# Two first loads placed ahead of their engines' register set-up, in a convolution with a residual add

## The chip, the cores and the metric

The kernel runs on one core of one Trainium2 chip. The metric is the device time of one execution in microseconds (us), lower is better. A run counts as slow here when its time is more than 1.5% above the fastest of the same kernel.

## The reference

A 3x3 convolution with padding 1, 16 images of 64 channels and 64x64 points to 64 channels, and then a residual added:

```python
"x": np.random.randn(16, 64, 64, 64).astype(np.float32),
"weight": np.random.randn(64, 64, 3, 3).astype(np.float32) * 0.1,
"residual": np.random.randn(16, 64, 64, 64).astype(np.float32),
...
output[b, co] += weight[co, ci, kh, kw] * x_pad[b, ci, kh:kh+h, kw:kw+w]
...
return (output + residual).astype(np.float32)
```

## The kernel before

SyncE issues the image loads, the weights, the residual loads and the stores; ScalarE issues the first residual load, and packs images as bf16; TensorE multiplies; VectorE adds the residual in place. The part that matters here is how two loads are issued. Each is issued as any other, then a helper takes it out of its place and inserts it into the first block of the program, ahead of the barrier with which all engines begin:

```python
def to_the_front(dma):
    ...
    front = nc.main_func.blocks[0].instructions
    here = nc.cur_bb.bb.instructions
    ins = here.pop()
    assert ins.name == dma.ins.name
    at = next(
        i for i, e in enumerate(front) if e.engine == ins.engine and isinstance(e, mybir.InstDrain)
    )
    front.insert(at, copy.replace(ins, ins=[fixed(a) for a in ins.ins], outs=[fixed(a) for a in ins.outs]))
...
# on SyncE
to_the_front(load_x(p))                       # the first image load, p == 0: 128 partitions x 16 KB
nc.sync.dma_start(out=wraw[:, :], in_=w_rows[:, :]).then_inc(s_w, 16)
...
# on ScalarE
to_the_front(load_ro(0, nc.scalar))           # the first residual load: 128 partitions x 16 KB
```

The first block, as printed while the kernel was traced, has for SyncE and ScalarE five register moves and a load of a base register each, then the barrier (a drain, a semaphore wait and a branch, of which the trace has records on all five engines). The drain is what the helper looks for.

## Time and profile before

| what | before |
|---|---|
| time, median (range) of 3 runs | 122.44 us (122.42 to 122.47) |
| span of the profiled run | 120.5 us |
| bytes moved, rate from 3.5 to 117 us | 50.48 MB, 431 GB/s |
| busiest compute engine | TensorE, 72% of the span |
| first image load, first residual load issued | 0.00 us, 0.12 us |
| first bytes | after 1.0 us |

The span counts from the first record, so a load at 0.00 us is itself that first record. Engine names with a q (SPq, ACTq) are the engines' sequencers, which issue transfers and run register, semaphore and branch instructions. In the lines of the profile PE is TensorE, DVE VectorE, ACT ScalarE, POOL GpSimd and SP SyncE; DMA stands for the 16 engines that carry the transfers; xr is the buffer of the images, ro that of the residual and the output, wraw that of the weights. The lines themselves stand in the prediction below.

### The profile page before, as it was taken

To read this page: it belongs to the slowest core of one execution; us is meant where nothing else is said; L and a number is where in the kernel's file an instruction comes from. 1 tells how busy PE (TensorE), PEld (TensorE's weight loads), DVE (VectorE), ACT (ScalarE), POOL (GpSimd) and SP (SyncE) were. 2 spreads that over 40 slices of the span, in tenths; PEclk is the share of its full clock that TensorE was granted. 3 is DMA by queue.
4 is the path that set the end of the run, shared out by engine and by line. 5 is a ranking of instruction groups with operands and counts; after the bars stand their busy time and mean duration, and the time that the engine had idled before them with its cause. 6 is when DMAs were issued, how large, how long until landed. Compare 5 with 4: busy or idle time off the path is not lost.

```text
span 120.5 us, 734 instructions
## 1 busy us (share of the span) xinstructions
PE 86.5 (72%) x389; PEld 10.7 (9%) x105; DVE 76.0 (63%) x40; ACT 63.1 (52%) x37; POOL 2.4 (2%) x16
## 2 busy tenths in 40 slices
PE   0000609999999999999999999999999999000000
PEld 0000300111010101010101010101010100000000
DVE  0000180077989898898988989897898988860000
ACT  4002999999999665895865959577400000000000
POOL 5200000000000000000000000000000000000000
PEclk9999999999999999999999999999999999965555
DMA  7999999999999999999999999999999999999994
GB/s 239 413 435 430 430 430 430 430 435 430 430 424 424 435 430 435 424 435 435 430 435 435 435 435 402 432 454 430 435 430 430 430 424 435 419 430 430 421 427 185
DMA packets 3808, 50.48 MB, mean 419 GB/s; under 512 B 352, under 2 KB 480, under 8 KB 480
## 3 DMA queue, kind: packets, MB, share of 16 engines
q1 hardware_dynamic: 3664, 48.38, 94.3%
q10 hardware_dynamic: 144, 2.10, 4.1%
HBM read 33.70 MB, written 16.78 MB: 419 GB/s over the span
## 4 chain that ended last, share of the span: by engine, by line
PE 70%; DVEq 2%; DVE 2%; issue 0%
PE ps L101 53%; PE ps L100 17%; DVEq L144 2%; DVE ro L222 2%
## 5 line engine op out<-in xcount | busy, mean ns | idle before, releaser
L222 DVE TENSOR_TENSOR ro<-ps,ro 64x2048 f32<-64x2048 f32 x32 | 73.2, 2289 | 16.5 <-PE ps L101 16.0
L101 PE MATMUL ps<-xp,wl 128*128 128x504 bf16 (+1 forms) x288 | 79.1, 384 | 0.2
L192 ACT CAST xp<-xr 64x2048 bf16<-64x2048 f32 x16 | 30.3, 1896 | 21.2 <-DMA xr<-in_x_dram 11.3
L100 PE MATMUL ps<-xp,wl 128*128 128x504 bf16 (+1 forms) x92 | 35.4, 385 | 3.4 <-PEq L243 3.4
L196 ACT CAST xp<-xr 64x2048 bf16<-64x2048 f32 x16 | 30.4, 1898 | 0.4
L100 PEld LDWEIGHTS ps<-xp,wl 128*128 128x128 bf16 x96 | 9.5, 99 | 78.0 <-issue 78.0
L208 DVE CAST wl<-ps 32x192 bf16<-32x192 f32 x8 | 2.8, 348 | 14.8 <-PE ps L235 14.7
L235 PE MATMUL ps<-ident,wraw 128*32 128x128 f32 x9 | 2.1, 416 | 12.5 <-DMA wraw<-in_weight_dram 12.5
L235 PEld LDWEIGHTS ps<-ident,wraw 128*32 128x32 f32 x9 | 1.2, 141 | 12.9 <-issue 12.5
L192 ACT ACT_TABLE_LOAD x1 | 1.3, 1283 | 1.1 <-SPq L144 1.1
L201 ACT CAST wl<-ps 32x192 bf16<-32x192 f32 x4 | 1.2, 305 | 0.0
L179 POOL MEMSET xp<- 64x64 bf16 x4 | 0.6, 146 | 0.2
L178 POOL MEMSET xp<- 64x64 bf16 x4 | 0.6, 144 | 0.2
L167 POOL TENSOR_SCALAR_AFFINE_SELECT ident<-ident 128x128 f32<-128x128 f32 x1 | 0.3, 292 | 0.2 <-POOL ident L165 0.2
L181 POOL MEMSET wl<- 64x192 bf16 x1 | 0.3, 252 | 0.1
L180 POOL MEMSET wl<- 64x192 bf16 x1 | 0.3, 251 | 0.1
L165 POOL MEMSET ident<- 128x128 f32 x1 | 0.2, 204 | 0.7 <-SPq L144 0.7
L279 POOL MEMSET const-bfloat16-1.0<- 128x1 bf16 x1 | 0.1, 111 | 0.0
L279 POOL MEMSET const-uint8-127<- 128x1 uint8 x1 | 0.1, 111 | 0.0
L279 POOL MEMSET const-float32-1.0<- 128x1 f32 x1 | 0.1, 108 | 0.0
L279 POOL MEMSET const-float32-0.0<- 128x1 f32 x1 | 0.1, 103 | 0.2 <-issue 0.2
## 6 DMA issues: line engine op xcount, KB each, us to landing
xr<-in_x_dram SPq DMA_DIRECT2D x8, 2048.0 KB, 14.8
out_dram<-ro SPq DMA_DIRECT2D x3, 4096.0 KB, 20.4
ro<-in_residual_dram SPq DMA_DIRECT2D x2, 4096.0 KB, 21.1
ro<-in_residual_dram SPq DMA_DIRECT2D x2, 2048.0 KB, 18.7
ro<-in_residual_dram ACTq DMA_DIRECT2D x1, 2048.0 KB, 12.0
ro<-in_residual_dram SPq DMA_DIRECT2D x2, 1024.0 KB, 19.4
out_dram<-ro SPq DMA_DIRECT2D x1, 2048.0 KB, 14.8
out_dram<-ro SPq DMA_DIRECT2D x2, 1024.0 KB, 10.6
```

The costliest lines, as they stand in the source:

```text
L100: return e.matmul(out=out_, lhsT=lhsT, rhs=rhs, start=start, stop=stop, skip_group_check=True)
L101: return e.add_instruction(mybir.InstMatmult(name=nc.get_next_instruction_name(), engine=PE, ins=[e.lower_ap(rhs), e.lower_ap(lhsT)], outs ...
L144: with tc.tile_critical(no_gpsimd_drain=True):
L178: nc.gpsimd.memset(t[0:64, 0, :], 0.0).then_inc(s_id, 1)
L179: nc.gpsimd.memset(t[64:128, J, :], 0.0).then_inc(s_id, 1)
L192: i = nc.scalar.copy(out=t[64:128, 0:J, :], in_=x4[hp, :, 0, :])
L196: nc.scalar.copy(out=t[0:64, 1 : J + 1, :], in_=x4[hp, :, 1, :]).then_inc(s_pack, 1)
L201: i = nc.scalar.copy(**weight_block(h, *b))
L208: i = nc.vector.tensor_copy(**weight_block(h, *b))
L222: i = nc.vector.tensor_tensor(out=o4[hp, :, par, :], in0=psj[64 * par : 64 * par + 64, :, :], in1=o4[hp, :, par, :], op=ADD)
L235: i = nc.tensor.transpose(out=tp[0:32, t // 3, 128 * (t % 3) : 128 * (t % 3) + 128], in_=wraw3[:, :, t], identity=ident[:, :])
L279: nc = _bacc.Bacc("TRN2", target_bir_lowering=False, num_devices=1)
```

## The change

The intent is to start the first two transfers sooner: they are to be the very first instructions of SyncE and ScalarE, ahead of the register set-up and no longer behind it. The diff, whole:

```diff
         assert ins.name == dma.ins.name
-        at = next(
-            i for i, e in enumerate(front) if e.engine == ins.engine and isinstance(e, mybir.InstDrain)
-        )
+        at = next(i for i, e in enumerate(front) if e.engine == ins.engine)
         front.insert(at, copy.replace(ins, ins=[fixed(a) for a in ins.ins], outs=[fixed(a) for a in ins.outs]))
```

## The prediction

> **What bounds the kernel now.** I read the page first from its table of forty slices, because a change to the first instructions can only pay if the end of the kernel hangs on its start.
>
> ```profile
> span 120.5 us, 734 instructions
> PE 86.5 (72%) x389; PEld 10.7 (9%) x105; DVE 76.0 (63%) x40; ACT 63.1 (52%) x37; POOL 2.4 (2%) x16
> ...
> DMA  7999999999999999999999999999999999999994
> GB/s 239 413 435 430 430 430 430 430 435 430 430 424 424 435 430 435 424 435 435 430 435 435 435 435 402 432 454 430 435 430 430 430 424 435 419 430 430 421 427 185
> DMA packets 3808, 50.48 MB, mean 419 GB/s; under 512 B 352, under 2 KB 480, under 8 KB 480
> ```
>
> No compute engine is busy for more than 72% of the span, while the DMA row is 9 in every slice but the first (7) and the last (4). So the transfers are the bound, and the chain of waits, which gives 70% to TensorE, shows only what ended last among the instructions, not what limits the kernel. The second reading is the table of stretches, taken finely at both ends (columns: busy time and count of each engine, granted clock, DMA share, GB/s):
>
> ```profile
> 0.00:0.50 0.50, 0.00 (x0) 0.00 (x0) 0.00 (x0) 0.00 (x0) 0.21 (x4) 1.00 0.00 0
> 0.50:1.00 0.50, 0.00 (x0) 0.00 (x0) 0.00 (x0) 0.00 (x0) 0.00 (x0) 1.00 0.00 0
> 1.00:1.50 0.50, 0.00 (x0) 0.00 (x0) 0.00 (x0) 0.43 (x1) 0.20 (x1) 1.00 1.77 426
> ...
> 3.50:117.00 113.50, 86.52 (x389) 10.67 (x105) 76.02 (x40) 61.83 (x36) 0.49 (x2) 0.95 1.01 431
> ...
> 118.50:119.00 0.50, 0.00 (x0) 0.00 (x0) 0.00 (x0) 0.00 (x0) 0.00 (x0) 0.50 0.59 246
> 119.00:119.50 0.50, 0.00 (x0) 0.00 (x0) 0.00 (x0) 0.00 (x0) 0.00 (x0) 0.50 0.01 0
> ```
>
> From 3.5 to 117 us the engines move 431 GB/s without a gap. All 50.48 MB at that rate take 50,480 / 431 = 117.1 us. The other 120.5 - 117.1 = 3.4 us of the span are about 1.0 us before the first bytes, some 0.5 us lost to thinner flow between 1.0 and 3.5 us (2.5 us less the 0.85 MB moved there at 431 GB/s), and about 1.7 us after the last bytes near 118.8 us; together 3.2 us, the rest is rounding. So a first transfer that is issued earlier by t should shorten the time by about t: this part of the idea behind the change is sound, one for one. The third reading is therefore the timeline of the start (start us, duration us, engine, line, what it does):
>
> ```profile
> 0.00 0.38 SPq L82 DMA_DIRECT2D xr<-in_x_dram  x1
> 0.12 0.36 ACTq L88 DMA_DIRECT2D ro<-in_residual_dram  x1
> 0.23 0.10 POOL L279 MEMSET const-float32-0.0<- 128x1 f32 x1 [0.23 <-issue]
> ...
> 1.07 1.28 ACT L192 ACT_TABLE_LOAD   x1 [1.07 <-SPq L144]
> 1.11 0.33 SPq L152 DMA_DIRECT2D wraw<-in_weight_dram  x1
> ```
>
> The reader is to see that in the kernel before, the load on SyncE is already the record that opens the span, at 0.00 us, and the one on ScalarE stands at 0.12 us; no register-setting record stands ahead of either. The page warns that register instructions aren't counted as busy, so this alone doesn't prove that there are none.
>
> [...]
>
> **The change part by part.** The edit alters one search. The helper takes the DMA just issued out of its place and inserts it into the first block of the program. Before, it went ahead of its engine's first drain; now it goes ahead of the first instruction of any kind of its engine. I printed that block while each kernel was traced. On each of SyncE and ScalarE, what stands between the two places is six instructions: five register moves and one load of a base register. So at this stage the edit really does jump over 6 instructions per engine, 12 in all; it adds none and removes none.
>
> But this list is not what runs. In the program as built, those twelve are gone: the build drops what sets a register that nothing reads, and nothing of SyncE or ScalarE here reads one (of the whole program only two register moves stay, one on TensorE for its loop and one on GpSimd, and neither engine is concerned). With them gone, the two places coincide: on SyncE and ScalarE the DMA is the first instruction of the built program, directly ahead of the drain, in both kernels. I compared the built programs engine by engine, instruction by instruction with all fields but the source line: SyncE 43 instructions, ScalarE 57, VectorE 62, TensorE 130, GpSimd 47, all equal and in equal order. What differs is how the lists of the five engines are interleaved in the first block (the two DMAs now stand above GpSimd's memsets in the text)[...]. I also compiled both and compared the five engines' streams byte for byte: identical[...]. Only the debug tables differ, as the kernel's later lines move up by two.
>
> So the sum is: instructions jumped over on the path, 0 x any duration = 0.00 us; instructions added, 0; semaphores, transfers, buffers, clock: the same. The change lies on the path that sets the end, and its size there is zero.
>
> **The rivals.**
> First rival: the set-up instructions survive after all, and the DMA gains their time. For it speaks the intent of the change, and that the page does not count register instructions. Against it speak the built streams, and the 0.00 us at which the load already starts. Its size, if true: short sequencer instructions in this trace last 7 to 51 ns (drains 7 to 49 ns, semaphore instructions 17 to 51 ns, on the lines of the barriers); six of them at an estimated 30 ns, from those records, are 0.2 us, and one for one that makes 122.44 - 0.2 = 122.2 us, -0.15%.
> [...]
> Third rival: the earlier load collides with something and costs time: [...]would push the weights back, whose landing lets TensorE start at 12.5 us. Against it: order and addresses are those of before, byte for byte[...]. Its time would be 122.4 to 122.8 us, as TensorE is idle for 28% anyway.
> Fourth rival, the only one I take seriously: nothing but spread between executions. The three runs of before lie within 0.05 us (122.42 to 122.47), the profiled run took 122.36.
>
> **Range and chances.** The prediction is the time before, 122.44 us. For the range I take the spread of the runs, 0.05 us, and the profiled run's -0.08 us, and allow for another session or another chip with some 0.2 us to both sides (my choice; the runs do not show it): 122.24 to 122.66 us. The first rival ends at the lower edge of that. For 2% either way the time would have to pass 120.0 or 124.9 us[...]: 0.4% of chance to each side, 99.2% for the same.
>
> **What would show each step right or wrong.** Right: in the profile after, the load on SyncE again opens the span at 0.00 us and lasts about 0.38 us; the load on ScalarE follows by about 0.1 us; the first barrier ends near 1.0 us, so that the weights are issued near 1.1 us; 734 instructions, 3808 packets and 50.48 MB; 431 GB/s in the middle; a span of 120.5 us within 0.3, and time minus span again near 1.9 us (122.36 - 120.5). Lines are numbered two lower. The first rival would show as a longer gap between the load on SyncE and the barrier's end, by some 0.2 us, as six instructions would now stand between them[...]. The prediction would be wrong if the streams on the chip were not those I compared, or if two executions of an equal program differed by more than the three before did.

What rested on something other than the traces and runs of this case is cut from this text and from one expectation below, and each cut is marked. The sum: 0.00 us for the change, 122.44 us for the time, 122.24 to 122.66 us for the range. That the middle of the kernel can't be sped up was not shown; that it moves 431 GB/s was. When the weights are issued: with a second load ahead of the barrier on SyncE (e8_small_first and e10_cols_first below) they were issued at 1.47 us and not at 1.11, so the loads have a part in it.

## The result, and the profile after

The changed kernel took 122.41 us (median of 4 runs, 122.28 to 122.44), the kernel before 122.43 us (median of 4 runs, 122.35 to 122.47). The ratio is 0.9997, with a 95% interval of 0.998 to 1.0014: the same. Ratios here and below are not quite the ratios of the medians quoted beside them. All outputs are right.

The page of the kernel after:

```profile
span 120.6 us, 734 instructions
PE 87.7 (73%) x389; PEld 10.7 (9%) x105; DVE 76.0 (63%) x40; ACT 63.1 (52%) x37; POOL 2.4 (2%) x16
...
DMA  7999999999999999999999999999999999999994
...
DMA packets 3808, 50.48 MB, mean 419 GB/s; under 512 B 352, under 2 KB 480, under 8 KB 480
```

The instructions, the packets, the bytes and the DMA row are those of before. The table of stretches of the kernel after (length, busy time of each engine, granted clock, DMA share, GB/s), at the start, in the middle and at the end:

```profile
0.50:1.00 0.50, 0.00 (x0) 0.00 (x0) 0.00 (x0) 0.00 (x0) 0.00 (x0) 1.00 0.00 0
1.00:1.50 0.50, 0.00 (x0) 0.00 (x0) 0.00 (x0) 0.43 (x1) 0.20 (x1) 1.00 1.87 426
...
3.50:117.00 113.50, 87.69 (x389) 10.68 (x105) 76.01 (x40) 61.83 (x36) 0.49 (x2) 0.96 1.01 431
...
118.50:119.00 0.50, 0.00 (x0) 0.00 (x0) 0.00 (x0) 0.00 (x0) 0.00 (x0) 0.50 0.59 246
```

And its timeline at the start (start, duration, engine, line, what):

```profile
0.00 0.38 SPq L82 DMA_DIRECT2D xr<-in_x_dram  x1
0.12 0.36 ACTq L88 DMA_DIRECT2D ro<-in_residual_dram  x1
0.23 0.10 POOL L277 MEMSET const-float32-0.0<- 128x1 f32 x1 [0.23 <-issue]
...
1.11 0.33 SPq L150 DMA_DIRECT2D wraw<-in_weight_dram  x1
```

GpSimd's first memset, which the change doesn't touch, serves as a clock of its own: it follows the image load by 0.23 us in both kernels. Had the load moved earlier against the other engines, this gap would have grown.

One difference shows how little TensorE matters: in this execution its work took 87.7 us and not 86.5, and the first of the last three stores that wait for it was issued at 101.11 us and not at 99.85, yet the bytes ended in the same half microsecond: at that moment other transfers were still in flight (431 GB/s from 3.5 to 117 us in both kernels).

### The profile page after: what moved, and what is told of

The parts are those of the page before. It is cut to its first block, busy times and chain, and to the rows that moved or that the text cites. A ratio compares the mean times of both kernels' runs of the same rounds, so it can differ in the third digit from the quotient of the medians.

```text
span 120.6 us, 734 instructions
## 1 busy us (share of the span) xinstructions
PE 87.7 (73%) x389; PEld 10.7 (9%) x105; DVE 76.0 (63%) x40; ACT 63.1 (52%) x37; POOL 2.4 (2%) x16
## 2 busy tenths in 40 slices
DMA packets 3808, 50.48 MB, mean 419 GB/s; under 512 B 352, under 2 KB 480, under 8 KB 480
## 4 chain that ended last, share of the span: by engine, by line
PE 71%; DVEq 2%; DVE 2%; issue 0%
PE ps L101 54%; PE ps L100 17%; DVEq L142 2%; DVE ro L220 2%
## 5 line engine op out<-in xcount | busy, mean ns | idle before, releaser
L101 PE MATMUL ps<-xp,wl 128*128 128x504 bf16 (+1 forms) x288 | 80.0, 388 | 0.2
L100 PE MATMUL ps<-xp,wl 128*128 128x504 bf16 (+1 forms) x92 | 35.9, 390 | 3.4 <-PEq L241 3.4
```

The source lines that it names most:

```text
L100: return e.matmul(out=out_, lhsT=lhsT, rhs=rhs, start=start, stop=stop, skip_group_check=True)
L101: return e.add_instruction(mybir.InstMatmult(name=nc.get_next_instruction_name(), engine=PE, ins=[e.lower_ap(rhs), e.lower_ap(lhsT)], outs ...
```

## The experiments

The question they have to answer is why an edit that jumps over six instructions on each of two engines did nothing. My theory is that these instructions are not in the program that runs. The rivals: the set-up is there but costs nothing, or an earlier first transfer is hidden behind something else. All runs were of five rounds against the kernel before, which gave four to six executions each, in three batches on three chips, each batch with its own runs of the kernel before. The edit of e2_kept_before is of the kernel before; all others are of the changed kernel. Where loads are delayed on purpose, register moves do it.

**The changed kernel again (e1_again).** No edit.

> The changed kernel once more, unaltered, for the size of the noise. My theory (the streams of all five engines are equal to those of the kernel before, so the change does nothing): ratio to the kernel before 1.000 within 0.15%, 122.3 to 122.5 us, first load at 0.00 us, ScalarE's at 0.12 us, weights issued at 1.11 us. The rival (the set-up instructions run somewhere and the load gained their time): a steady gain of some 0.2 us, ratio 0.998, whose interval leaves out 1.

Measured: 122.35 us (122.28 to 122.5), before 122.34 us, ratio 0.9994, interval 0.9981 to 1.0008. A steady gain of 0.2 us (0.998) lies outside the interval by a hair, no gain at all well inside. Such an interval is about 0.14% or 0.17 us to each side; what follows can't be read finer than that.

**The set-up kept, with the loads behind it (e2_kept_before) and ahead of it (e3_kept_after).** To both kernels I added an instruction that reads the registers of the set-up, so that the build doesn't drop it (the traces below show it there). The first is the kernel before with this addition, the second the changed kernel with it, so the two differ by the change alone.

```diff
+    def keep_setup(e):
+        front = nc.main_func.blocks[0].instructions
+        here = nc.cur_bb.bb.instructions
+        kinds = ("InstRegisterMove", "InstTPBBaseLd")
+        regs = [o for x in front if x.engine == e.engine and type(x).__name__ in kinds for o in x.outs]
+        e.keepalive_nop(regs)
+        at = next(i for i, x in enumerate(front) if x.engine == e.engine and isinstance(x, mybir.InstDrain))
+        front.insert(at, here.pop())
...
                 to_the_front(load_x(p))
+                keep_setup(nc.sync)
...
         to_the_front(load_ro(0, nc.scalar))
+        keep_setup(nc.scalar)
```

> The premise of the change restored, at the place of the kernel before: an instruction that reads them keeps the six set-up instructions (five register moves and one base load) of SyncE and of ScalarE in the built program, ahead of the first load. If the set-up had been in the kernel before all along (rival), this changes nothing: 122.43 us, and the gap from the load to the weights' issue stays 1.11 us. If it had been dropped (my theory), six instructions more stand ahead of the load and all transfers start later: at an estimated 30 ns each (short sequencer instructions took 7 to 51 ns in the trace of before) 0.2 us more, 122.6 us, ratio 1.0016; the load's own record is then no longer the first of SyncE, or the gap from the start of GpSimd's first memset (at 0.23 us after the load) to the load shrinks.

> The same six instructions kept, with the change applied, so that the load stands ahead of them: what the change was meant to be. My theory: the load starts as in the kernel before, the six run behind it under a queue that holds 4 MB, so 122.43 us within 0.1 (the first barrier and the weights' issue come some 0.2 us later, at 1.1 to 1.4 us, which is hidden, because 4 MB take 9.7 us at 431 GB/s). The difference of this run and of the one with the six ahead of the load is what the change would have been worth: 0.2 us expected. The rival, that a later barrier shows in the time: 122.6 us as well, no difference between the two.

Measured: loads behind the set-up 122.78 us (122.74 to 122.95), ratio to the kernel before 1.0033 (1.0019 to 1.0047); loads ahead of it 122.42 us (122.3 to 122.63), ratio 1.0006 (0.9992 to 1.0019). The view of all records of one source line settles where the set-up is. The moves, the base load, the drain and the semaphore wait that the framework puts into the first block have one line (the branch behind them has another, L290). In the kernel before it is L279, and these are all its records on SyncE and ScalarE (count, then shortest, median and longest in ns, then the first and last start in us):

```profile
L279 SPq DRAIN  x1: 131/131/131, 0.4 to 0.4; - x1
L279 ACTq DRAIN  x1: 145/145/145, 0.5 to 0.5; - x1
L279 SPq EVENT_SEMAPHORE  x1: 17/17/17, 0.8 to 0.8; - x1
L279 ACTq EVENT_SEMAPHORE  x1: 17/17/17, 0.8 to 0.8; - x1
```

In the run with the set-up kept ahead of the loads, the same line (there it is numbered L290) has these besides:

```profile
L290 SPq MOVE  x5: 29/29/40, 0.0 to 0.3; - x5
L290 ACTq MOVE  x5: 29/29/39, 0.1 to 0.4; - x5
...
L290 SPq BASE_LOAD  x1: 12/12/12, 0.1 to 0.1; - x1
...
L290 ACT BASE_LOAD  x1: 12/12/12, 0.2 to 0.2; - x1
```

So the profiler does record moves, five per engine with one base load, where the program has them; on this line neither the kernel before nor the changed one has a single one. The timeline of the run with the set-up kept ahead shows the loads put off:

```profile
0.38 0.38 SPq L82 DMA_DIRECT2D xr<-in_x_dram  x1
0.48 0.38 ACTq L88 DMA_DIRECT2D ro<-in_residual_dram  x1
```

The memset, at 0.23 us in the kernel before and at 0.24 us here, lets the two clocks be compared: the image load starts 0.37 us later. (The 1.11 us from the load to the weights' issue, named in the expectation beside the rival, stayed as well, from 0.38 to 1.49 us; with the set-up ahead of the load it stays under either theory, and so decides nothing.) The time grew by 0.33% of 122.34 us, 0.40 us. With the load ahead of the set-up the loads are back at 0.00 and 0.12 us, the weights' issue is put off to 1.41 us (by 0.30 us, the sign that the prediction had named for set-up behind the load), and the time is that of before within the noise. The difference of the two, 1.0033 - 1.0006 = 0.27% or 0.33 us, is what the change is worth in a kernel that still has its set-up; the intervals leave some 0.2 us to each side of it, but no run of the one lies within the range of the other. This confirms the theory, and its size was 0.33 us where I had expected 0.2.

**Neither load moved to the front (e4_late).** `to_the_front(load_x(p))` becomes `load_x(p)`, and the same for the residual load.

> Both loads left where they are issued, behind the first barrier, none moved to the front. If the time depends one for one on when the first transfer is issued, the loads start at about 1.1 us on the clock of before, 1.1 us later, and the time is 123.5 us, ratio 1.009. The rival (the start is hidden, as TensorE first waits for weights and has 28% of idle time): 122.4 us.

Measured: 123.64 us (123.58 to 123.73), ratio 1.01 (1.0084 to 1.0115), 1.22 us more. In the timeline the loads follow the barrier:

```profile
0.24 0.10 POOL L277 MEMSET const-float32-0.0<- 128x1 f32 x1 [0.24 <-issue]
...
0.91 0.39 ACTq L88 DMA_DIRECT2D ro<-in_residual_dram  x1
0.95 0.38 SPq L82 DMA_DIRECT2D xr<-in_x_dram  x1
```

The image load is 0.94 us later than before and the residual load 0.78 us, so the start is not hidden; 1.22 us (give or take 0.17) is somewhat more than one for one. The stretches tell where: by 5 us the engines had moved 223 GB/s x 5 us, against 311 in the kernel before, which is 0.44 MB or 1.02 us at 431 GB/s. The rest fits an uneven end, with a DMA share of 0.12, two of sixteen engines' worth, still busy between 120.0 and 120.5 us. I have not tested that part.

**Sixteen live moves ahead of both loads (e5_moves_both), of one load (e6_moves_sp, e7_moves_act), and behind both (e9_moves_behind).**

```diff
+    def delay(e, n):
+        ...
+        regs = [e.alloc_register(f"delay{i}") for i in range(n)]
+        for i, r in enumerate(regs):
+            e.reg_mov(r, 1000 + i)
+        e.keepalive_nop([e.lower_val_access(r) for r in regs])
+        # taken out of their place and inserted ahead of the engine's first instruction
+        # (in the run with the moves behind: one place further on)
...
                 to_the_front(load_x(p))
+                delay(nc.sync, 16)        # not in the run on ScalarE alone
...
         to_the_front(load_ro(0, nc.scalar))
+        delay(nc.scalar, 16)              # not in the run on SyncE alone
```

> Sixteen register moves that an instruction reads, so that the build keeps them, ahead of the first load on SyncE and on ScalarE. In the run with the six set-up instructions kept ahead, six put the load off by 0.38 us, 0.063 us each, so sixteen should put it off by 1.0 us. If the time follows the first issue one for one: 122.34 + 1.0 = 123.35 us, ratio 1.0082. The rival, that only the fixed cost of having any such instruction counts: 122.8 us as with six.

> The sixteen moves on SyncE alone; the residual load on ScalarE stays the first of its engine. Theory that the DMA engines only need something to carry: ScalarE's 2.1 MB occupy them for 4.9 us at 431 GB/s, so the image load may come 1.0 us later without loss: 122.35 to 122.5 us. Rival: what counts is the arrival of the first images for the packing on ScalarE, or one queue alone can't fill the engines: 122.7 to 123.3 us.

> The sixteen moves on ScalarE alone; the image load on SyncE stays first. Same theory: 2.1 MB of images occupy the engines for 4.9 us, 122.35 to 122.5 us, and so either load alone at the front gives nearly the whole of what both give. Rival: two queues are needed for the full rate at the start, then up to 0.5 us more, 122.8 us.

> The sixteen register moves behind the load on SyncE and on ScalarE, so that both loads start as in the kernel before (0.00 and 0.12 us), but the first barrier, the weights' issue and all later issues come some 0.9 us later, at about 2.0 us, as in the run with sixteen ahead on ScalarE alone. If the 0.6 us of the two one-sided runs came from the one load that was late, this takes 122.4 us, within 0.1. If it came from the later barrier (rival), 123.0 us, ratio 1.005, as they took.

Measured, with the image and the residual load's issue from the timelines, and the rate from 0 to 5 us:

| kernel | image load | residual load | rate, 0 to 5 us | time | ratio to before (95%) |
|---|---|---|---|---|---|
| before (both batches) | 0.00 us | 0.12 us | 311 GB/s | 122.38, 122.30 us | 1 |
| ahead of both | 0.88 us | 1.04 us | 210 GB/s | 123.67 us | 1.011 (1.0096 to 1.0125) |
| ahead on SyncE | 0.88 us | 0.14 us | 265 GB/s | 122.94 us | 1.005 (1.0035 to 1.0065) |
| ahead on ScalarE | 0.00 us | 1.03 us | 275 GB/s | 123.03 us | 1.0052 (1.0039 to 1.0065) |
| behind both | 0.00 us | 0.12 us | 315 GB/s | 122.58 us | 1.0022 (1.0009 to 1.0036) |

The rates come from these lines of the tables of stretches, in the order of the table:

```profile
0.00:5.00 5.00, 0.00 (x0) 0.00 (x0) 0.00 (x0) 1.28 (x1) 2.37 (x16) 1.00 0.83 311
```

```profile
0.00:5.00 5.00, 0.00 (x0) 0.00 (x0) 0.00 (x0) 1.28 (x1) 2.38 (x16) 1.00 0.62 210
```

```profile
0.00:5.00 5.00, 0.00 (x0) 0.00 (x0) 0.00 (x0) 1.28 (x1) 2.37 (x16) 1.00 0.78 265
```

```profile
0.00:5.00 5.00, 0.00 (x0) 0.00 (x0) 0.00 (x0) 1.28 (x1) 2.37 (x16) 1.00 0.82 275
```

```profile
0.00:5.00 5.00, 0.00 (x0) 0.00 (x0) 0.00 (x0) 1.28 (x1) 2.38 (x16) 1.00 0.84 315
```

Four things follow.

First, the delay goes with the number of live moves: six instructions put the image load off by 0.37 us, sixteen moves by 0.87 us (0.88 less the 0.01 us by which the memset stands later), 54 ns each, where I had expected 1.0 us. The rival of a fixed cost, 122.8 us, falls.

Second, the same sixteen moves cost 1.011 - 1.0022 = 0.88%, 1.08 us, more ahead of both loads than behind them, for a shift of 0.87 to 0.91 us: again one for one or a little more.

Third, I was wrong about the one-sided runs: I expected either load alone to occupy the engines, and each run lost about 0.6 us. The run with the moves behind separates two causes of that. It has similarly late weights (issued at 1.90 us, against 1.88 and 2.04 us), but both loads in time, and it lost 0.27 us. So some 0.28% to 0.30%, 0.34 to 0.37 us, is due to the one late load, give or take some 0.2 us, and with the reservation that here both engines carry moves. It is not the packing of the first images that counts: with the image load late the first packing began at 12.7 us, with the residual load late at 10.2 us (11.4 us in the kernel before), and both lost the same. The stretch from 2 to 3 us, in the kernel before and then with the one load late on SyncE and on ScalarE, shows where the bytes are missing:

```profile
2.00:3.00 1.00, 0.00 (x0) 0.00 (x0) 0.00 (x0) 0.35 (x1) 0.73 (x6) 1.00 1.12 459
```

```profile
2.00:3.00 1.00, 0.00 (x0) 0.00 (x0) 0.00 (x0) 1.00 (x1) 0.66 (x4) 1.00 0.59 213
```

```profile
2.00:3.00 1.00, 0.00 (x0) 0.00 (x0) 0.00 (x0) 1.00 (x1) 0.64 (x3) 1.00 0.74 279
```

Up to 2 us one load alone moved about as much as both (123 and 131 GB/s on average, against 131 in the kernel before), and from 3 us on the rates are alike again (434 and 418, against 418 GB/s up to 5 us). So here one load started the flow as well as two did, and the gap comes behind that; what sets it was not tested, nor were both loads on one engine.

Fourth, the 0.27 us of the moves behind both lies between the two times I had named, and is not explained: the bytes flow in the first 5 us as before (315 and 311 GB/s), and I found no stretch that loses them.

**The first load in two pieces, by partitions (e8_small_first) and by columns (e10_cols_first).** The one thing left at the start is the 1.0 us from the issue to the first bytes.

```diff
-                to_the_front(load_x(p))
+                rest, first = slice(16, 128), slice(0, 16)
+                for rows in (rest, first):
+                    to_the_front(nc.sync.dma_start(out=xr[0][rows, :], in_=x_bc[rows, :]).then_inc(s_x[0], 16))
...
-                nc.scalar.wait_ge(s_x[p % NXR], 16 * (p // NXR + 1))
+                nc.scalar.wait_ge(s_x[p % NXR], 16 * (p // NXR + 1 + (p % NXR == 0)))
```

The second piece issued goes ahead of the first, so the small one leads. By columns the slices are 1024 to 4096 and 0 to 1024, of all 128 partitions.

> A try at the part of the head that is left: the first image load is issued in two pieces, 16 partitions (0.26 MB) and then 112, both at the front, since the record of the load lasts 0.38 us and bytes flow only from 1.0 us. [...]if the latency does not depend on the size, 122.35 us; if the second issue puts off what follows and the uneven pieces cost rate, up to 122.6 us.

> The first image load in two pieces again, but cut by columns: 128 partitions of 1024 columns (0.5 MB), then 128 of 3072. If the 4.25 us lost by the pieces of 16 and 112 partitions came from the cut by partitions, this takes 122.2 to 122.6 us; below 122.3 us only if smaller first rows make bytes flow earlier. If any second issue at the front costs this, some 126 us.

Measured: by partitions 126.63 us, ratio 1.0347 (1.0333 to 1.036); by columns 123.35 us, ratio 1.0082 (1.0068 to 1.0096). Both are losses, and both missed what I had expected (up to 122.6 us), so there is no version here that beats the kernel before. In the run by columns, with first rows of 4 KB where the kernel before has 16 KB, nothing moved from 0.8 to 1.0 us and the first bytes came from 1.0 to 1.2 us, as in the kernel before (there 0.6 to 0.8 us after the end of the load's record, which lasts 0.38 us). So this smaller first transfer did not make bytes flow sooner. The two issues took 0.86 us of SyncE, and by 5 us 247 GB/s had flowed on average against 311. The cut by partitions lost more, in the first 20 us:

```profile
0.00:5.00 5.00, 0.00 (x0) 0.00 (x0) 0.00 (x0) 1.28 (x1) 2.37 (x16) 1.00 0.83 210
5.00:10.00 5.00, 0.00 (x0) 0.00 (x0) 0.00 (x0) 0.00 (x0) 0.00 (x0) 1.00 1.03 341
10.00:20.00 10.00, 2.08 (x9) 1.16 (x9) 0.90 (x3) 3.57 (x2) 0.00 (x0) 1.00 0.99 342
```

In the kernel before, the last two stretches are:

```profile
5.00:10.00 5.00, 0.00 (x0) 0.00 (x0) 0.00 (x0) 0.00 (x0) 0.00 (x0) 1.00 0.99 423
10.00:20.00 10.00, 4.04 (x14) 1.45 (x11) 2.79 (x8) 8.46 (x8) 0.00 (x0) 1.00 1.02 434
```

Against 311, 423 and 434 GB/s that is 0.51 + 0.41 + 0.92 = 1.84 MB, which at 431 GB/s are 4.3 us, the whole of the 4.3 us lost. The DMA share is about as high as before (0.83, 1.03 and 0.99 against 0.83, 0.99 and 1.02) while the rate is lower, so the engines were busy but slower. A second issue alone doesn't cost this: by columns the loss was 0.82%, 1.0 us. The other 3.2 us or so go with the cut by partitions; but the two cuts differ in the size of the first piece too (0.26 and 0.5 MB), and by what mechanism the bytes slow down I did not test.

## Why the prediction was right

- **The bound.** The prediction rested the end on the transfers. That held: with loads later by 0.94 us the time rose by 1.22 us, and TensorE's 1.2 us more of work in the run after hardly showed (122.44 us against 122.36 in the two profiled executions).
- **The streams are equal.** This was read off the built programs, and the chip agreed twice: ratios 0.9997 and 0.9994. The runs with the set-up kept showed the cause from the trace: five moves and a base load per engine where it is kept, none before and none after, and with them kept the same edit is worth 0.33 us.
- **The signs.** Image load at 0.00 us for 0.38 us, residual load at 0.12 us, weights at 1.11 us, 734 instructions, 3808 packets, 431 GB/s: all as said. Time less span was 122.44 - 120.6 = 1.8 us, where 1.9 had been named.
- **The first rival.** It was rightly set aside, but its term was too small. I sized six set-up instructions at an estimated 30 ns each, 0.2 us, from how long the records of short instructions last. (The "7 to 49 ns" for drains also leaves out those directly behind the two loads, 131 and 145 ns in the lines above.) A move's record lasts 29 ns in the median, yet six instructions put the load off by 0.37 us, 62 ns each, twice the record. Had the set-up been there, the change would have brought 0.33 us, and 122.1 us would have been below my range.
- **The open doubt.** I wrote that the absence of register records on the page proves nothing. That was true of the page, but the view by source line lists them: in the kernel before it has the one move left on GpSimd (L167) and the one on TensorE (L240), and none on L279. So the trace of before alone could have answered it.
- **The rate.** From 20 to 60 us it was 430 to 433 GB/s in every run. Single slices of 3 us go above that (up to 454 in the kernel before), and why is not shown.

## What to carry to other kernels

Before sizing an edit that moves instructions, compare what each engine runs in the built program, not what the traced list says: what the edit jumps over may already be gone, as were twelve instructions here (five moves and a base load recorded per engine where they were kept, none in the kernel before). In this kernel, bound by its transfers from end to end, each microsecond by which the first loads started later cost about a microsecond or a little more (1.22 us for 0.94 and 0.78 us, 1.08 us for 0.87 and 0.91 us), and one of the two late by 0.9 us cost some 0.35 us; that an earlier start than the present one would pay as much is likely by this, but no run shows it. The step that paid here, moving the loads ahead of the first barrier (1.2 us), had been taken before this change.
